# Hardware loops with lowered semaphores, and a first store in one piece, in a LayerNorm + GELU kernel

## The chip, the cores and the metric

The kernel runs on one core of a Trainium2 chip. The metric is the device time of one execution in microseconds (us), as a median over several executions. A profile of one execution shows each engine's instructions and each DMA packet; its span is 1.8 to 2.2 us shorter than the device time of that execution. The page is the profile's summary, and the chain is the work that ended last, followed back step by step to what released it. Engines: TensorE (PE, weight loads PEld), VectorE (DVE), ScalarE (ACT), GpSimd (POOL), SyncE (SP); a q behind a name is the engine's sequencer.

## The reference

The input `x` is 8 x 1024 rows of 2048 float32 values. Each row is normalised, scaled, shifted and put through the tanh form of GELU.

```python
mean = np.mean(x, axis=-1, keepdims=True)
var = np.var(x, axis=-1, keepdims=True)
normalized = (x - mean) / np.sqrt(var + eps)
out = gamma * normalized + beta
return (0.5 * out * (1 + np.tanh(np.sqrt(2 / np.pi) * (out + 0.044715 * out ** 3)))).astype(np.float32)
```

It reads 67.1 MB and writes 67.1 MB, and each value is used once.

## The kernel before

8192 rows make 64 tiles of 128 rows, in 16 batches of four tiles (4 MB). Five batch buffers go round. SyncE loads a batch as soon as the store from that buffer has landed. For each tile VectorE takes the statistics, GpSimd makes 1/sqrt(var + eps) and the shift from them, ScalarE normalises into bf16, VectorE multiplies by gamma, TensorE adds beta in PSUM (one matmul group puts beta there, the second adds the tile through an identity), and ScalarE applies GELU and writes over the batch buffer, which is then stored. All is unrolled in Python. The kernel's semaphores only rise, so each wait has its own number.

```python
def by_row(b):
    return b in (0, B - 1)            # first and last batch: stored as four 1 MB rows
# SyncE
for b in range(B):
    s = b % SLOTS
    if b >= SLOTS:
        prev = sum(16 * (R if by_row(c) else 1) for c in range(s, b, SLOTS))
        sy.wait_ge(s_store[s], prev)
    if b == 0:
        for q in range(R):
            sy.dma_start(out=xts[0][:, q:q + 1], in_=xg[0, :, q:q + 1]).then_inc(s_first[q], 16)
    else:
        sy.dma_start(out=xts[s], in_=xg[b]).then_inc(s_load[s], 16)
# ... GpSimd, unrolled over 64 tiles, three instructions each ...
# VectorE
for t in range(1, T):
    stats(t)          # four bn_stats, one bn_aggr
    scale(t - 1)      # times gamma; scale(0) first waits until gamma is spread: ve.wait_ge(s_c, 3)
scale(T - 1)
# ... ScalarE ...
# TensorE
for i in range(T):
    ps = pss[i % 2]
    for j in range(nsub):
        ins = pe.matmul(ps[:, cols(j)], lhsT=ones_b, rhs=b_hl[:, cols(j)], start=True, stop=False)
        if j == 0 and i >= 2:
            ins._wait_ge(s_g, i - 1)
    for j in range(nsub):
        ins = pe.matmul(ps[:, cols(j)], lhsT=ident, rhs=zgs[i % 2][:, cols(j)], start=False, stop=True)
        if j == 0:
            ins._wait_ge(s_v, v_scale(i))
    ins.then_inc(s_t, 1)
```

## Time and profile before

| | before |
|---|---|
| device time, median of 3 | 320.23 us (320.16 to 320.3) |
| span of the profile | 318.7 us |
| busiest engine | ScalarE, 79% |
| DMA, middle of the run | busy all the time, 425 to 432 GB/s |
| data moved | 134.36 MB in 6010 packets |
| pace of batches, loads at hand / in the long run | 16.4 / 19.4 us |

The prediction shows the lines behind this table and how they are read. In short: the DMA row has 9 (90% or more) in all slices but the ends, no engine has, and the waits are all of the kind "a buffer is not stored yet" or "a load is not here yet".

### The profile page before, as it was taken

The numbers are of one execution on the slowest core, as the hardware profiler recorded it, in microseconds if no ns is written. First come the engines' busy times: TensorE is split into PE (matmuls) and PEld (weight loads), VectorE is DVE, ScalarE is ACT, GpSimd is POOL, SyncE is SP. The second block draws the span as 40 slices with busy tenths as digits, with TensorE's granted clock in tenths as the row PEclk, the third lists the DMA queues.
The fourth block names the chain that finished last, engine by engine and source line by source line (L and its number), as shares of the span: only waits on it lengthen the run. The fifth ranks groups of instructions, "written<-read, shape, count | busy, mean of one in ns | idle before, by whom it ended". The sixth has DMA issues, their size and how long they took to land.

```text
span 318.7 us, 1855 instructions
## 1 busy us (share of the span) xinstructions
PE 241.2 (76%) x510; PEld 57.2 (18%) x520; DVE 249.1 (78%) x386; ACT 252.9 (79%) x132; POOL 115.1 (36%) x201
## 2 busy tenths in 40 slices
PE   2788889889989989785895868859687786768830
PEld 1211112222222222121121111112121121112100
DVE  3688999999999997996869868598786978968610
ACT  2779999999999999796896959949598696977850
POOL 1133444444444444333434424243232452433400
DMA  7999999999999999999999999999999999999995
GB/s 287 440 456 396 427 428 453 409 449 391 411 448 415 449 432 422 441 419 452 419 440 436 419 444 419 446 428 428 444 416 448 419 441 440 415 450 415 448 394 223
DMA packets 6010, 134.36 MB, mean 422 GB/s; under 512 B 704, under 2 KB 752, under 8 KB 752
## 3 DMA queue, kind: packets, MB, share of 16 engines
q1 hardware_dynamic: 2736, 67.11, 49.4%
q10 hardware_dynamic: 3264, 67.14, 49.1%
q8 instruction: 4, 0.07, 0.1%
q14 instruction: 6, 0.05, 0.0%
HBM read 67.13 MB, written 67.11 MB: 421 GB/s over the span
## 4 chain that ended last, share of the span: by engine, by line
DMA 63%; ACT 15%; DVE 9%; POOL 5%; PE 3%; issue 1%; ACTq 1%; SPq 0%
DMA out_dram<-xt 34%; DMA xt<-in_x_dram 27%; ACT yk L178 9%; DVE sts L143 6%; ACT xt L182 5%; POOL rss L131 3%; DVE zg L154 2%; PE ps L196 2%; DMA rows<-in_gamma_dram 2%; POOL ves L129 2%; POOL nms L133 1%; DVE mvs L149 1%; ACT g_t L175 1%; PE ps L210 1%; ACTq L187 0%
## 5 line engine op out<-in xcount | busy, mean ns | idle before, releaser
L143 DVE BATCH_NORM_STATS2 sts<-xt 128x6 f32<-128x512 f32 x256 | 157.7, 678 | 28.9 <-DMA xt<-in_x_dram 28.8
L178 ACT ACTIVATE yk<-xt,nms,rss 128x2048 bf16<-128x2048 f32 x64 | 133.9, 2092 | 44.9 <-POOL nms L133 39.9
L210 PE MATMUL ps<-zg,ident 128*128 128x512 bf16 x246 | 117.7, 627 | 57.2 <-DVE zg L154 55.6
L206 PE MATMUL ps<-b_hl,ones_b 33*128 33x512 bf16 x256 | 120.6, 624 | 2.0 <-ACT g_t L175 2.0
L182 ACT ACTIVATE xt<-ps 128x2048 f32<-128x2048 f32 x64 | 118.8, 1857 | 2.4 <-PE ps L210 2.4
L154 DVE TENSOR_TENSOR zg<-yk,g_t 128x2048 bf16<-128x2048 bf16 x64 | 77.3, 1208 | 20.8 <-ACT yk L178 20.8
L129 POOL TENSOR_SCALAR ves<-mvs 128x1 f32<-128x1 f32 x64 | 29.0, 454 | 172.9 <-DVE mvs L149 172.9
L131 POOL TENSOR_TENSOR rss<-ves,mhalf 128x1 f32<-128x1 f32 x64 | 55.5, 868 | 5.3
L210 PEld LDWEIGHTS ps<-zg,ident 128*128 128x128 bf16 x256 | 27.6, 130 | 147.3 <-DVE zg L154 112.0
L206 PEld LDWEIGHTS ps<-b_hl,ones_b 33*128 33x128 bf16 x256 | 27.1, 127 | 91.9 <-issue 88.4
L133 POOL TENSOR_SCALAR nms<-mvs,rss 128x1 f32<-128x1 f32 x64 | 29.6, 462 | 6.3
L149 DVE BATCH_NORM_AGGREGATE mvs<-sts 128x2 f32<-128x24 f32 x64 | 16.8, 263 | 2.2
L196 PE MATMUL ps<-rows,ones 1*128 1x512 f32 x8 | 7.2, 1072 | 6.1 <-DMA rows<-in_gamma_dram 6.1
L173 ACT ACTIVATE b_hl<-rows 1x2048 bf16<-1x2048 f32 x1 | 1.9, 1908 | 5.1 <-DMA rows<-in_beta_dram 5.1
L160 DVE TENSOR_TENSOR b_hl<-rows,b_hl 1x2048 bf16<-1x2048 f32 x1 | 2.3, 2280 | 2.5 <-ACT b_hl L174 2.5
L196 PEld LDWEIGHTS ps<-rows,ones 1*128 1x128 f32 x8 | 2.5, 322 | 9.3 <-DMA rows<-in_gamma_dram 6.1
L175 ACT ACTIVATE g_t<-ps 128x2048 bf16<-128x2048 f32 x1 | 1.9, 1877 | 2.2 <-PE ps L196 2.2
L169 ACT ACT_TABLE_LOAD x1 | 1.3, 1283 | 0.9 <-SPq L105 0.9
L174 ACT ACTIVATE b_hl<-rows 1x2048 bf16<-1x2048 f32 x1 | 1.9, 1908 | 0.0
L157 DVE MEMSET b_hl<- 33x1024 uint32 x1 | 0.9, 912 | 1.2 <-SPq L105 1.2
L121 POOL MEMSET ones<- 65x128 f32 x1 | 0.2, 201 | 0.5 <-SPq L105 0.5
L125 POOL TENSOR_SCALAR_AFFINE_SELECT ident<-ident 128x128 bf16<-128x128 bf16 x1 | 0.3, 292 | 0.1
(7 smaller groups left out, 0.9 us busy)
## 6 DMA issues: line engine op xcount, KB each, us to landing
xt<-in_x_dram SPq DMA_DIRECT2D x15, 4096.0 KB, 29.1
out_dram<-xt ACTq DMA_DIRECT2D x14, 4096.0 KB, 37.6
out_dram<-xt ACTq DMA_DIRECT2D x8, 1024.0 KB, 14.6
xt<-in_x_dram SPq DMA_DIRECT2D x4, 1024.0 KB, 8.4
rows<-in_beta_dram ACTq DMA_DIRECT2D x2, 8.0 KB, 5.8
rows<-in_gamma_dram ACTq DMA_DIRECT2D x1, 8.0 KB, 5.2
```

The source lines that it names most:

```text
L129: po.tensor_scalar(out=ves[:, c], in0=mvs[:, i, 1:2], scalar1=float(eps), scalar2=1.0, op0=ALU.add, op1=ALU.mult)._wait_ge(s_v, v_stats(i) ...
L131: po.tensor_tensor(out=rss[:, c], in0=ves[:, c], in1=mhalf, op=ALU.pow)._wait_ge(s_p, 3 * i + 1).then_inc(s_p, 1)
L133: po.tensor_scalar(out=nms[:, c], in0=mvs[:, i, 0:1], scalar1=rss[:, c], scalar2=-1.0, op0=ALU.mult, op1=ALU.mult)._wait_ge(s_p, 3 * i + 2 ...
L143: ins = ve.bn_stats(out=sts[:, i, j, :], in_=xr[:, j, :])
L149: ve.bn_aggr(out=mvs[:, i], in_=sts[:, i])._wait_ge(s_v, v_stats(i) - 1).then_inc(s_v, 1)
L154: ve.tensor_tensor(out=zgs[i % 2], in0=yks[i % 2], in1=g_t, op=ALU.mult)._wait_ge(s_n, i + 1).then_inc(s_v, 1)
L175: ac.activation(out=g_t, in_=pss[0], func=ACT.Identity)._wait_ge(s_tg, 1).then_inc(s_c, 1)
L178: ac.activation(out=yks[t % 2], in_=xrow(t), func=ACT.Identity, scale=rss[:, t:t + 1], bias=nms[:, t:t + 1])._wait_ge(s_p, 3 * t + 3).then ...
L182: ac.activation(out=xrow(i), in_=pss[i % 2], func=ACT.Gelu_apprx_tanh)._wait_ge(s_t, i + 1).then_inc(s_g, 1)
L196: ins = pe.matmul(pss[0][:, cols(j)], lhsT=ones[64:65], rhs=rows[64:65, j * K // nsub:(j + 1) * K // nsub, :d // K], start=True, stop=True)
L206: ins = pe.matmul(ps[:, cols(j)], lhsT=ones_b, rhs=b_hl[:, cols(j)], start=True, stop=False)
L210: ins = pe.matmul(ps[:, cols(j)], lhsT=ident, rhs=zgs[i % 2][:, cols(j)], start=False, stop=True)
```

## The change

Three engines no longer run straight-line code. VectorE loops 3 times over five batches, TensorE and GpSimd 16 times over one. A loop body has the same wait numbers in every turn, so a looped engine lowers the semaphores that it waits on by the count of the turn (VectorE a load's at once, the others at the end of the turn). The programme gets shorter; before fetches its instructions in ten packets (four on q8, six on q14), and the hope was for fewer. For five equal batches per turn the buffers are renumbered so that batch 0 stands alone. Two transfers change with it: the first batch is stored in one 4 MB piece, and batch 3 is loaded in four 1 MB pieces. From batch 1 on a load raises its semaphore by 64 in all. Cut to the core:

```diff
-        return b in (0, B - 1)
+        return b == B - 1                       # by_row
...
+                    elif b == SPLIT:            # SPLIT = 3
+                        sy.dma_start(out=xts[s][:, q:q + 1], in_=xg[b, :, q:q + 1]).then_inc(s_load[s], 16)
+                if b not in (0, SPLIT):
+                    sy.dma_start(out=xts[s], in_=xg[b]).then_inc(s_load[s], 16 * R)
...                                              # GpSimd
-        for i in range(T):
+            with po.Fori(0, B):
+                for k in range(R):
...
+                po.sem_inc(s_a, -R)
+                po.sem_inc(s_q, -2 * R)
...                                              # VectorE
+                if q == 0:
+                    ...
+                    ve.wait_ge(s_c, 3)
+                else:
+                    scale(q - 1, q)
...
+            with ve.Fori(0, (B - 1) // SLOTS):
+                for k in range(SLOTS * R):
+                    s, q = divmod(k, R)
+                    stats(s, q, (s_load[s], 16 * R) if q == 0 else None, k + 1)
+                    scale((q - 1) % R, k + 1)
+                ve.sem_inc(s_o, -SLOTS * R)
+                ve.sem_inc(s_n, -SLOTS * R)
...                                              # TensorE
+            pe.sem_inc(s_g, 2)
+            with pe.Fori(0, B):
+                for k in range(R):
...                                              # the eight matmuls as before
+                pe.sem_inc(s_g, -R)
+                pe.sem_inc(s_z, -R)
```

More of the change, by code (lines that the diff above doesn't have):

```diff
@@ L12 @@
 SLOTS = 5
+SPLIT = 3
+K = 16
 @with_exitstack
@@ L34 @@
     B = T // R
+    assert (B - 1) % SLOTS == 0
     xg = xf.rearrange("(b p r) d -> b p r d", p=P, r=R)
@@ L50 @@
     pss = [psum.tile([P, d], f32, name=f"ps{s}") for s in range(2)]
-    K = 16
     rows = sb("rows", [65, K, d // K + 4], f32)
@@ L58 @@
     g_t = sb("g_t", [P, d], bf16)
-    sts = sb("sts", [P, T, nsub, nc.vector.BN_STATS_DIM], f32)
-    mvs = sb("mvs", [P, T, 2], f32)
-    ves = sb("ves", [P, T], f32)
-    rss = sb("rss", [P, T], f32)
-    nms = sb("nms", [P, T], f32)
+    sts = sb("sts", [P, R, nsub, nc.vector.BN_STATS_DIM], f32)
+    mvs = sb("mvs", [P, R, 2], f32)
+    ves = sb("ves", [P, R], f32)
+    rss = sb("rss", [P, R], f32)
+    nms = sb("nms", [P, R], f32)
     def sem(name):
@@ L73 @@
     s_setp = sem("setp")
-    s_v = sem("v")
+    s_m = sem("m")
+    s_o = sem("o")
+    s_a = sem("a")
+    s_z = sem("z")
+    s_q = sem("q")
     s_p = sem("p")
@@ L77 @@
     s_g = sem("g")
+    s_r = sem("r")
     s_c = sem("c")
@@ L80, with slot @@
     s_tg = sem("tg")
-    def xrow(i):
-        return xts[i // R % SLOTS][:, i % R]
+    def slot(b):
+        return (b + SLOTS - 1) % SLOTS
     def row(p):
@@ L92, in cols @@
         return slice(j * FMAX, (j + 1) * FMAX)
-    def v_stats(t):
-        return 3 if t == 0 else 4 + 2 * t + (t - 1)
-    def v_scale(t):
-        return v_stats(t + 1) + 1 if t + 1 < T else v_stats(T - 1) + 2
     def by_row(b):
-        return b in (0, B - 1)
-    with tc.tile_critical():
-        sy = nc.sync
-        for b in range(B):
-            s = b % SLOTS
-            if b >= SLOTS:
-                prev = sum(16 * (R if by_row(c) else 1) for c in range(s, b, SLOTS))
-                sy.wait_ge(s_store[s], prev)
-            if b == 0:
-                for q in range(R):
-                    sy.dma_start(out=xts[0][:, q:q + 1], in_=xg[0, :, q:q + 1]).then_inc(s_first[q], 16)
-            else:
-                sy.dma_start(out=xts[s], in_=xg[b]).then_inc(s_load[s], 16)
-        po = nc.gpsimd
-        po.memset(ones, 1.0)
-        po.memset(ones_b, 1.0)
-        po.memset(mhalf, -0.5)
-        po.memset(ident, 0.0).then_inc(s_setp, 1)
-        po.affine_select(out=ident, in_=ident, compare_op=ALU.not_equal, fill=1.0, base=0,
-                         pattern=[[-1, P]], channel_multiplier=1)._wait_ge(s_setp, 1).then_inc(s_setp, 1)
-        for i in range(T):
-            c = slice(i, i + 1)
-            po.tensor_scalar(out=ves[:, c], in0=mvs[:, i, 1:2], scalar1=float(eps), scalar2=1.0,
-                             op0=ALU.add, op1=ALU.mult)._wait_ge(s_v, v_stats(i)).then_inc(s_p, 1)
-            po.tensor_tensor(out=rss[:, c], in0=ves[:, c], in1=mhalf,
-                             op=ALU.pow)._wait_ge(s_p, 3 * i + 1).then_inc(s_p, 1)
-            po.tensor_scalar(out=nms[:, c], in0=mvs[:, i, 0:1], scalar1=rss[:, c], scalar2=-1.0,
-                             op0=ALU.mult, op1=ALU.mult)._wait_ge(s_p, 3 * i + 2).then_inc(s_p, 1)
-        ve = nc.vector
-        def stats(i):
-            xr = xrow(i).rearrange("p (s f) -> p s f", f=FMAX)
-            b, q = divmod(i, R)
-            for j in range(nsub):
-                ins = ve.bn_stats(out=sts[:, i, j, :], in_=xr[:, j, :])
-                if j == 0 and b == 0:
-                    ins._wait_ge(s_first[q], 16)
-                elif j == 0 and q == 0:
-                    ins._wait_ge(s_load[b % SLOTS], 16 * (b // SLOTS + (b % SLOTS > 0)))
-            ins.then_inc(s_v, 1)
-            ve.bn_aggr(out=mvs[:, i], in_=sts[:, i])._wait_ge(s_v, v_stats(i) - 1).then_inc(s_v, 1)
-        def scale(i):
-            if i == 0:
-                ve.wait_ge(s_c, 3)
-            ve.tensor_tensor(out=zgs[i % 2], in0=yks[i % 2], in1=g_t,
-                             op=ALU.mult)._wait_ge(s_n, i + 1).then_inc(s_v, 1)
-        ve.memset(b_hl, 0.0).then_inc(s_v, 1)
-        stats(0)
-        ve.tensor_tensor(out=split(b_hl[32:33]), in0=row(32), in1=split(b_hl[32:33]),
-                         op=ALU.subtract)._wait_ge(s_c, 2).then_inc(s_v, 1)
-        for t in range(1, T):
-            stats(t)
-            scale(t - 1)
-        scale(T - 1)
-        ac = nc.scalar
-        ac.preload_act_table(ACT.Gelu_apprx_tanh)
-        for k, (p, src) in enumerate(((64, gamma), (0, beta), (32, beta))):
-            ac.dma_start(out=row(p), in_=src.rearrange("(o k f) -> o k f", o=1, k=K)).then_inc(s_par[k], 16)
-        ac.wait_ge(s_v, 1)
-        ac.activation(out=split(b_hl[0:1]), in_=row(0), func=ACT.Identity)._wait_ge(s_par[1], 16).then_inc(s_c, 1)
-        ac.activation(out=split(b_hl[32:33]), in_=row(32), func=ACT.Identity)._wait_ge(s_par[2], 16).then_inc(s_c, 1)
-        ac.activation(out=g_t, in_=pss[0], func=ACT.Identity)._wait_ge(s_tg, 1).then_inc(s_c, 1)
-        for t in range(T + 1):
-            if t < T:
-                ac.activation(out=yks[t % 2], in_=xrow(t), func=ACT.Identity, scale=rss[:, t:t + 1],
-                              bias=nms[:, t:t + 1])._wait_ge(s_p, 3 * t + 3).then_inc(s_n, 1)
-            i = t - 1
-            if i >= 0:
-                ac.activation(out=xrow(i), in_=pss[i % 2],
-                              func=ACT.Gelu_apprx_tanh)._wait_ge(s_t, i + 1).then_inc(s_g, 1)
-                b, q = divmod(i, R)
-                s = b % SLOTS
-                if by_row(b):
-                    ac.dma_start(out=og[b, :, q:q + 1],
-                                 in_=xts[s][:, q:q + 1])._wait_ge(s_g, i + 1).then_inc(s_store[s], 16)
-                elif q == R - 1:
-                    ac.dma_start(out=og[b], in_=xts[s])._wait_ge(s_g, i + 1).then_inc(s_store[s], 16)
-        pe = nc.tensor
-        pe.wait_ge(s_setp, 2)
-        for j in range(nsub):
-            ins = pe.matmul(pss[0][:, cols(j)], lhsT=ones[64:65],
-                            rhs=rows[64:65, j * K // nsub:(j + 1) * K // nsub, :d // K], start=True, stop=True)
-            if j == 0:
-                ins._wait_ge(s_par[0], 16)
-        ins.then_inc(s_tg, 1)
-        pe.wait_ge(s_c, 3)
-        pe.wait_ge(s_v, 4)
-        for i in range(T):
-            ps = pss[i % 2]
-            for j in range(nsub):
-                ins = pe.matmul(ps[:, cols(j)], lhsT=ones_b, rhs=b_hl[:, cols(j)], start=True, stop=False)
-                if j == 0 and i >= 2:
-                    ins._wait_ge(s_g, i - 1)
-            for j in range(nsub):
-                ins = pe.matmul(ps[:, cols(j)], lhsT=ident, rhs=zgs[i % 2][:, cols(j)], start=False, stop=True)
-                if j == 0:
-                    ins._wait_ge(s_v, v_scale(i))
-            ins.then_inc(s_t, 1)
-        for s in range(SLOTS):
-            sy.wait_ge(s_store[s], sum(16 * (R if by_row(c) else 1) for c in range(s, B, SLOTS)))
@@ new lines, in by_row, with stored, _, stats @@
+        return b == B - 1
+    def stored(b):
+        return sum(16 * (R if by_row(c) else 1) for c in range(b) if slot(c) == slot(b))
+    with tc.tile_critical(), nc.Block() as block:
+        @block.sync
+        def _(sy):
+            for b in range(B):
+                s = slot(b)
+                if stored(b):
+                    sy.wait_ge(s_store[s], stored(b))
+                for q in range(R):
+                    if b == 0:
+                        sy.dma_start(out=xts[s][:, q:q + 1], in_=xg[0, :, q:q + 1]).then_inc(s_first[q], 16)
+                    elif b == SPLIT:
+                        sy.dma_start(out=xts[s][:, q:q + 1], in_=xg[b, :, q:q + 1]).then_inc(s_load[s], 16)
+                if b not in (0, SPLIT):
+                    sy.dma_start(out=xts[s], in_=xg[b]).then_inc(s_load[s], 16 * R)
+            for b in range(B, B + SLOTS):
+                sy.wait_ge(s_store[slot(b)], stored(b))
+        @block.gpsimd
+        def _(po):
+            po.memset(ones, 1.0)
+            po.memset(ones_b, 1.0)
+            po.memset(mhalf, -0.5)
+            po.memset(ident, 0.0).then_inc(s_setp, 1)
+            po.affine_select(out=ident, in_=ident, compare_op=ALU.not_equal, fill=1.0, base=0,
+                             pattern=[[-1, P]], channel_multiplier=1)._wait_ge(s_setp, 1).then_inc(s_setp, 1)
+            with po.Fori(0, B):
+                for k in range(R):
+                    c = slice(k, k + 1)
+                    po.tensor_scalar(out=ves[:, c], in0=mvs[:, k, 1:2], scalar1=float(eps), scalar2=1.0,
+                                     op0=ALU.add, op1=ALU.mult)._wait_ge(s_a, k + 1).then_inc(s_q, 1)
+                    po.tensor_tensor(out=rss[:, c], in0=ves[:, c], in1=mhalf,
+                                     op=ALU.pow)._wait_ge(s_q, 2 * k + 1).then_inc(s_q, 1)
+                    po.tensor_scalar(out=nms[:, c], in0=mvs[:, k, 0:1], scalar1=rss[:, c], scalar2=-1.0,
+                                     op0=ALU.mult, op1=ALU.mult)._wait_ge(s_q, 2 * k + 2).then_inc(s_p, 1)
+                po.sem_inc(s_a, -R)
+                po.sem_inc(s_q, -2 * R)
+        @block.vector
+        def _(ve):
+            def stats(s, q, wait, count):
+                xr = xts[s][:, q].rearrange("p (s f) -> p s f", f=FMAX)
+                for j in range(nsub):
+                    ins = ve.bn_stats(out=sts[:, q, j, :], in_=xr[:, j, :])
+                    if j == 0 and wait:
+                        ins._wait_ge(*wait)
+                        if wait[0] is s_load[s]:
+                            ins.then_inc(s_load[s], -16 * R)
+                ins.then_inc(s_o, 1)
+                ve.bn_aggr(out=mvs[:, q], in_=sts[:, q])._wait_ge(s_o, count).then_inc(s_a, 1)
+            def scale(q, count):
+                ve.tensor_tensor(out=zgs[q % 2], in0=yks[q % 2], in1=g_t,
+                                 op=ALU.mult)._wait_ge(s_n, count).then_inc(s_z, 1)
+            ve.memset(b_hl, 0.0).then_inc(s_m, 1)
+            for q in range(R):
+                stats(slot(0), q, (s_first[q], 16), q + 1)
+                if q == 0:
+                    ve.tensor_tensor(out=split(b_hl[32:33]), in0=row(32), in1=split(b_hl[32:33]),
+                                     op=ALU.subtract)._wait_ge(s_c, 2).then_inc(s_m, 1)
+                    ve.wait_ge(s_c, 3)
+                else:
+                    scale(q - 1, q)
+            ve.sem_inc(s_o, -R)
+            ve.sem_inc(s_n, -(R - 1))
+            with ve.Fori(0, (B - 1) // SLOTS):
[5 more added lines that the diff above has]
+                ve.sem_inc(s_n, -SLOTS * R)
+            scale(R - 1, 1)
+        @block.scalar
+        def _(ac):
+            ac.preload_act_table(ACT.Gelu_apprx_tanh)
+            for k, (p, src) in enumerate(((64, gamma), (0, beta), (32, beta))):
+                ac.dma_start(out=row(p), in_=src.rearrange("(o k f) -> o k f", o=1, k=K)).then_inc(s_par[k], 16)
+            ac.wait_ge(s_m, 1)
+            ac.activation(out=split(b_hl[0:1]), in_=row(0), func=ACT.Identity)._wait_ge(s_par[1], 16).then_inc(s_c, 1)
+            ac.activation(out=split(b_hl[32:33]), in_=row(32),
+                          func=ACT.Identity)._wait_ge(s_par[2], 16).then_inc(s_c, 1)
+            ac.activation(out=g_t, in_=pss[0], func=ACT.Identity)._wait_ge(s_tg, 1).then_inc(s_c, 1)
+            for t in range(T + 1):
+                if t < T:
+                    b, q = divmod(t, R)
+                    ac.activation(out=yks[t % 2], in_=xts[slot(b)][:, q], func=ACT.Identity, scale=rss[:, q:q + 1],
+                                  bias=nms[:, q:q + 1])._wait_ge(s_p, t + 1).then_inc(s_n, 1)
+                i = t - 1
+                if i < 0:
+                    continue
+                b, q = divmod(i, R)
+                xt = xts[slot(b)]
+                ins = ac.activation(out=xt[:, q], in_=pss[i % 2], func=ACT.Gelu_apprx_tanh)._wait_ge(s_t, i + 1)
+                if by_row(b):
+                    ins.then_inc(s_r, 1)
+                    ac.dma_start(out=og[b, :, q:q + 1], in_=xt[:, q:q + 1])._wait_ge(
+                        s_r, b + q + 1).then_inc(s_store[slot(b)], 16)
+                    ac.sem_inc(s_g, 1)
+                elif q == R - 1:
+                    ins.then_inc(s_r, 1)
+                    ac.dma_start(out=og[b], in_=xt)._wait_ge(s_r, b + 1).then_inc(s_store[slot(b)], 16)
+                    ac.sem_inc(s_g, 1)
+                else:
+                    ins.then_inc(s_g, 1)
+        @block.tensor
+        def _(pe):
+            pe.wait_ge(s_setp, 2)
+            for j in range(nsub):
+                ins = pe.matmul(pss[0][:, cols(j)], lhsT=ones[64:65],
+                                rhs=rows[64:65, j * K // nsub:(j + 1) * K // nsub, :d // K], start=True, stop=True)
+                if j == 0:
+                    ins._wait_ge(s_par[0], 16)
+            ins.then_inc(s_tg, 1)
+            pe.wait_ge(s_c, 3)
+            pe.wait_ge(s_m, 2)
+            pe.sem_inc(s_g, 2)
+            with pe.Fori(0, B):
+                for k in range(R):
+                    ps = pss[k % 2]
+                    for j in range(nsub):
+                        ins = pe.matmul(ps[:, cols(j)], lhsT=ones_b, rhs=b_hl[:, cols(j)], start=True, stop=False)
+                        if j == 0:
+                            ins._wait_ge(s_g, k + 1)
+                    for j in range(nsub):
+                        ins = pe.matmul(ps[:, cols(j)], lhsT=ident, rhs=zgs[k % 2][:, cols(j)],
+                                        start=False, stop=True)
+                        if j == 0:
+                            ins._wait_ge(s_z, k + 1)
+                    ins.then_inc(s_t, 1)
+                pe.sem_inc(s_g, -R)
+                pe.sem_inc(s_z, -R)
```

## The prediction

> **What bounds the kernel now.** I read the page first: its engine shares, its 40 slices and its DMA queues.
>
> ```profile
> PE 241.2 (76%) x510; PEld 57.2 (18%) x520; DVE 249.1 (78%) x386; ACT 252.9 (79%) x132; POOL 115.1 (36%) x201
> ...
> DMA  7999999999999999999999999999999999999995
> ...
> DMA packets 6010, 134.36 MB, mean 422 GB/s; under 512 B 704, under 2 KB 752, under 8 KB 752
> ...
> q1 hardware_dynamic: 2736, 67.11, 49.4%
> q10 hardware_dynamic: 3264, 67.14, 49.1%
> q8 instruction: 4, 0.07, 0.1%
> q14 instruction: 6, 0.05, 0.0%
> ```
>
> No engine is over 79%, and the 16 DMA engines are at 9 in every slice but the first and the last. q1 is the loads, q10 the stores, q8 and q14 fetch instructions. The table by stage shows how hard the bound is: the DMA share is 1.00 in the middle, at 425 to 432 GB/s.
>
> ```profile
> 24.00:56.00 32.00, 27.65 (x60) 6.40 (x60) 29.02 (x46) 29.43 (x16) 14.25 (x23) 1.00 1.00 425
> 56.00:120.00 64.00, 56.88 (x122) 13.37 (x126) 59.73 (x95) 59.18 (x32) 27.57 (x47) 1.00 1.01 427
> 120.00:200.00 80.00, 61.72 (x134) 14.40 (x134) 64.65 (x102) 64.95 (x35) 30.83 (x51) 1.00 1.00 432
> 200.00:280.00 80.00, 60.05 (x130) 14.10 (x132) 62.95 (x100) 63.26 (x34) 29.15 (x50) 1.00 1.00 432
> ```
>
> In the packet records a 32 KB packet takes 1.213 us and an 8 KB packet 0.309 us on its engine. There are 1920 + 1792 of 32 KB and 512 + 1024 of 8 KB: (3712 x 1.213 + 1536 x 0.309) / 16 = 311.1 us. All packets together, with the slow ones, are 314.1 us on each engine; the first data packet starts at 1.9 us and the last ends at 317.0 us. So the span of 318.7 us is 1.9 of head, 314 of DMA work without a hole that I could find (no stretch of 4 us between 4 and 312 us lost more than 0.15 us), and some 2.5 us of uneven finish and completion.
>
> The waits say how much room the compute has.
>
> ```profile
> SPq L117 <- DMA out_dram<-xt: 245.6, 11, 58.1
> ...
> DVE sts L143 <- DMA xt<-in_x_dram: 28.8, 10, 3.8
> ```
>
> SyncE waits for stores to free buffers, and VectorE waits for loads. While loads lie ready, the batch stores are issued at 52.6, 69.3, 85.6, 101.9 and 118.3 us, 16.4 us apart. That is the pace of compute. From 136 us on they are 19.4 us apart, which is 8.39 MB at 432 GB/s, the pace of DMA. The slack is thus 3.0 us in each batch.
>
> The end of the chain, in order of time, gives the second number that matters.
>
> ```profile
> 254.36 29.12 DMA xt<-in_x_dram
> 283.48 0.02 issue
> 283.50 2.48 DVE sts L143 x4
> ...
> 306.57 1.88 ACT xt L182
> ```
>
> The last load lands at 283.5 us and the last GELU ends 25 us later, at 308.45. The last row's store needs 8 x 0.309 = 2.5 us of DMA[...]. It ends near 317 because it queues behind earlier stores. So the tail too is set by DMA[...].
>
> [...]from 24 to 56 us the loads (32 KB packets) move some 340 GB/s and the row stores (8 KB) some 80, about 4 to 1; later, with equal packets, both get about 215. [...] The trace shows the blocks as q8 packets of 16 KB, four, 65 to 77 us apart (16 tiles of 16 TensorE instructions), and 8 KB ones on q14[...]. [...]
>
> **The change, part by part.**
>
> *Transfers.* The first store becomes one piece (four 8 KB-packet stores become one of 32 KB packets), and the load of batch 3 is cut into four (the reverse). 8 KB packets: loads 1024, stores 512, again 1536 in all; 32 KB again 3712. The sum stays 311.1 us: **0 us**.
>
> *Order of transfers.* The first store is issued at about 36 us, where its fourth row was, not 22.5. Until then loads run alone, 9.8 us a batch (measured 13.1 to 22.9 us for the second): three batches by 32.7 us, half of batch 3 by 37.5. Then a 32 KB store runs against 8 KB loads, 4 to 1, and needs 9.7 x 5/4 = 12.1 us: done by about 50 us, where the row stores ended at 62.5. Load 5 is issued near 51 instead of 63.4. Batch 3 is loaded by 52 us; store 1 begins at 54 and shares evenly with load 4, done by about 70; load 5, 19.4 us later, by about 89 (before: 87.3 by bytes). DMA has work throughout. All later loads move by some +2 us, the last one to land near 285.5. [...]**0 us**.
>
> *Loops.* VectorE turns back twice, TensorE and GpSimd 15 times. A turn is two semaphore instructions and a branch[...]. TensorE idles 57.2 us before its second matmul group, 0.9 us a tile, and GpSimd 172.9 us in 64 waits, 2.7 us; most of that covers a turn, and the 3.0 us slack per batch covers the rest: **0 us**. VectorE's body is 20 tiles x 6 = 120 instructions[...], with about 28 before it. Its 8 KB fetches before were at 42.9, 132.4 and 232.4 us (by their spacing of some 21 tiles); at 42.9 it was about 50 instructions in. [...]
>
> *Fewer fetches.* A fetch takes 0.31 us (8 KB) or 0.88 to 0.97 us (16 KB) on one DMA engine, and the next packet there took 0.4 to 0.55 us too long: 0.85 to 1.4 us each. [...] Four TensorE and about two GpSimd fetches go; one or two VectorE ones may come. I judge **-0.7 us** from the difference between engines that fetched 16 KB (ending 315.4 to 315.9) and most others (314.3 to 314.8); matching packets to engines was not certain.
>
> *Entry and exit.* [...] The extra issues on SyncE fall after enough is queued.
>
> Sum: 320.23 - 0.7 + 0.2, rounded to **319.7 us**.
>
> **Rivals.** [...] (2) The shifted order makes the last load later than I worked out[...] and compute ends the kernel: +1 to +3 us, 322 us. For it: the tail is short of spare time. Against it: +2 us is what the order gives. (3) All fetch delay falls away and the engines end level near 314.5: -2 us, 318 us. Against it: ScalarE remains unrolled and still fetches.
>
> **Range and chances.** Rivals 2 and 3 make the ends: **318.2 to 321.8 us**. Faster by 2% is under 313.8, below head plus DMA work, which the change leaves alone: 0.01. Slower by 2% is over 326.6, rival 1: 0.04. Same: 0.95.
>
> **What would show it.** Right: DMA at 9 in all slices but the ends; 6010 packets again; q8 with no or one fetch; the first store issued near 36 us, load 5 near 51; the last load landing at 285 to 286; the last GELU ending near 310 with stores still queued. Wrong: a gap in DMA or under 425 GB/s in the middle; TensorE idle for 3 us and more at the start of each batch; store issues more than 19.4 us apart; or a last store that starts as soon as it is issued.

The sum: 320.23 - 0.7 + 0.2 = 319.73, rounded to 319.7 us; the +0.2 us was for entry and exit, a guess that no trace gave. Rival 1, by which TensorE waits for instructions at every turn, is cut too; the 0.04 for "slower" rested on it. The blocks on q8 and q14 are the packets that the page calls instruction.

## The result and the profile after

The changed kernel took 320.65 us (median of 4 runs, 320.52 to 320.87), against 320.26 us for before beside it. The ratio is 1.0011 with a 95% interval of 0.9994 to 1.0028: the same. In two later comparisons the changed kernel was 0.06 us above and 0.09 us below before. The 0.5 us of gain that I had forecast did not come in any of the three.

The page of the changed kernel's profile, in the parts that answer to those shown of before:

```profile
PE 244.4 (77%) x520; PEld 57.2 (18%) x520; DVE 247.5 (78%) x386; ACT 251.7 (79%) x132; POOL 110.5 (35%) x201
...
DMA  7999999999999999999999999999999999999994
...
DMA packets 6002, 134.26 MB, mean 421 GB/s; under 512 B 704, under 2 KB 752, under 8 KB 752
...
q1 hardware_dynamic: 3168, 67.11, 49.4%
q10 hardware_dynamic: 2832, 67.13, 48.9%
q14 instruction: 2, 0.02, 0.0%
```

The busy times of the engines and the DMA row are nearly those of before. The packets only changed sides: 432 fewer on the stores' queue, 432 more on the loads', where the split first store and the now split load hand over 4 x 128 - 128 data packets and 3 x 16 small ones. The ten instruction fetches (q8 and q14) became two; the 6010 packets that I had named as a sign had not taken off these eight.

The stages of 24 to 56 and 56 to 120 us, in the columns of the prediction's table (the last two are the DMA share and GB/s):

```profile
24.00:56.00 32.00, 29.07 (x64) 6.55 (x61) 29.62 (x47) 29.67 (x16) 13.60 (x24) 1.00 1.00 414
56.00:120.00 64.00, 57.94 (x126) 13.53 (x127) 59.60 (x96) 59.11 (x32) 26.80 (x46) 1.00 1.00 433
```

Before had 425 and 427 GB/s there: the changed kernel moves less in the first stage, with DMA just as busy, and more in the second.

The waits of SyncE and VectorE of the changed kernel (total us, times, longest):

```profile
SPq L121 <- DMA out_dram<-xt: 241.4, 11, 46.6
...
DVE sts L151 <- DMA xt<-in_x_dram: 30.7, 11, 3.5
```

These are the waits of before with nearly the same totals (245.6 and 28.8 us). And the chain at its end, in order of time (start, duration, what):

```profile
251.85 31.78 DMA xt<-in_x_dram
283.64 0.03 issue
...
283.73 2.48 DVE sts L151 x4
...
307.04 1.88 ACT xt L204
```

The last load landed at 283.6 us (283.5 before) and the last GELU ended at 308.9 us (308.45 before). The load of batch 5 was issued at 53.3 us, where I had worked out 51 and before had 63.4.

Such a "same" can be nothing plus nothing, or a gain and a loss that meet. The experiments had to tell which.

### The profile page after: what moved, and what is told of

Read it like the earlier page. It is cut to its first block, busy times and chain, and to the rows that moved or that the text cites. A ratio compares the mean times of both kernels' runs of the same rounds, so it can differ in the third digit from the quotient of the medians.

```text
span 318.6 us, 2087 instructions
## 1 busy us (share of the span) xinstructions
PE 244.4 (77%) x520; PEld 57.2 (18%) x520; DVE 247.5 (78%) x386; ACT 251.7 (79%) x132; POOL 110.5 (35%) x201
## 4 chain that ended last, share of the span: by engine, by line
DMA 63%; ACT 14%; DVE 10%; POOL 5%; PE 3%; issue 1%; ACTq 0%; DVEq 0%; POOLq 0%; SPq 0%
DMA out_dram<-xt 31%; DMA xt<-in_x_dram 30%; ACT yk L197 9%; DVE sts L151 7%; ACT xt L204 4%; POOL ves L137 3%; DVE zg L160 2%; PE ps L222 2%; POOL rss L139 2%; DMA rows<-in_gamma_dram 2%; DVE mvs L157 1%; POOL nms L141 1%; PE ps L239 1%; ACT g_t L193 1%; ACTq L207 0%
## 5 line engine op out<-in xcount | busy, mean ns | idle before, releaser
L151 DVE BATCH_NORM_STATS2 sts<-xt 128x6 f32<-128x512 f32 x256 | 157.7, 679 | 32.1 <-DMA xt<-in_x_dram 30.7
L239 PE MATMUL ps<-zg,ident 128*128 128x512 bf16 x256 | 120.8, 627 | 54.6 <-DVE zg L160 53.5
L137 POOL TENSOR_SCALAR ves<-mvs 128x1 f32<-128x1 f32 x64 | 37.4, 585 | 177.9 <-DVE mvs L157 177.9
L160 DVE TENSOR_TENSOR zg<-yk,g_t 128x2048 bf16<-128x2048 bf16 x64 | 76.5, 1195 | 19.0 <-ACT yk L197 19.0
L139 POOL TENSOR_TENSOR rss<-ves,mhalf 128x1 f32<-128x1 f32 x64 | 37.1, 580 | 5.3
L141 POOL TENSOR_SCALAR nms<-mvs,rss 128x1 f32<-128x1 f32 x64 | 34.9, 546 | 6.3
```

The lines of the kernel that those rows point to most:

```text
L137: po.tensor_scalar(out=ves[:, c], in0=mvs[:, k, 1:2], scalar1=float(eps), scalar2=1.0, op0=ALU.add, op1=ALU.mult)._wait_ge(s_a, k + 1).the ...
L139: po.tensor_tensor(out=rss[:, c], in0=ves[:, c], in1=mhalf, op=ALU.pow)._wait_ge(s_q, 2 * k + 1).then_inc(s_q, 1)
L141: po.tensor_scalar(out=nms[:, c], in0=mvs[:, k, 0:1], scalar1=rss[:, c], scalar2=-1.0, op0=ALU.mult, op1=ALU.mult)._wait_ge(s_q, 2 * k + 2 ...
L151: ins = ve.bn_stats(out=sts[:, q, j, :], in_=xr[:, j, :])
L160: ve.tensor_tensor(out=zgs[q % 2], in0=yks[q % 2], in1=g_t, op=ALU.mult)._wait_ge(s_n, count).then_inc(s_z, 1)
L239: ins = pe.matmul(ps[:, cols(j)], lhsT=ident, rhs=zgs[k % 2][:, cols(j)], start=False, stop=True)
```

## The experiments

The theory was that DMA packets set the time, that their number and sizes have not changed, and that turns of the loops are hidden. Rivals: the new transfers cost something and the loops win it back; or the turns cost something. A third question was whether a turn of a loop can wait for its own instructions.

### One part of the change at a time

The new transfers on the unrolled kernel:

```diff
-        return b in (0, B - 1)
+        return b == B - 1
...
+            elif b == SPLIT:
+                for q in range(R):
+                    sy.dma_start(out=xts[s][:, q:q + 1], in_=xg[b, :, q:q + 1]).then_inc(s_load[s], 16)
```

> The unrolled kernel of before with the new transfers alone: first store in one piece, load of batch 3 in four. Theory (DMA packets set the time, their number and sizes are the same): 320.3 us, within 0.3 us of before; load 5 issued near 53 us, last load landing near 283.6 us, instruction packets on q8 four as before. Rival (the new order costs the 0.4 us that the changed kernel seems slower by, and the loops cost nothing): 320.6 to 320.7 us.

Measured: 320.76 us against 320.45 us for before on the same chip. Four of the six runs lie from 320.62 to 320.8; two took 322.98 and 324.77 us, for which no profile shows a reason, and they pull the ratio of the means to 1.0048 (1.0009 to 1.0086). So 0.3 us by the medians: the rival's side, not mine, though barely.

The loops with the transfers of before:

```diff
-SPLIT = 3
+SPLIT = 0                                  # batch 3 in one piece
...
-        return b == B - 1
+        return b in (0, B - 1)             # first batch in four rows
```

> The changed kernel with the transfers of before: first batch stored in four rows, batch 3 loaded in one piece. Theory: 320.3 us, within 0.3 us of before; load 5 issued near 63 us again; two or three instruction packets. Rival (the loops cost the 0.4 us): 320.6 to 320.7 us. A third (the missing instruction fetches are worth what I predicted, and the new order gives it back): 319.6 us.

Measured: 319.77 us, ratio 0.9981 (0.9968 to 0.9994). The third possibility came true: the loops are worth 0.7 us, and the new transfers give it back. The page of this kernel:

```profile
DMA packets 6002, 134.26 MB, mean 422 GB/s; under 512 B 704, under 2 KB 752, under 8 KB 752
...
q1 hardware_dynamic: 2736, 67.11, 49.3%
q10 hardware_dynamic: 3264, 67.14, 49.1%
q14 instruction: 2, 0.02, 0.0%
```

The data queues have exactly the packets of before; only the instruction queues differ, two fetches in place of ten.

> The changed kernel itself once more, as control on this chip beside the others. Theory: no difference to before that clears the noise, 320.3 to 320.7 us. Rival: a steady 0.4 us over before, with an interval that leaves out 1.

Measured: 320.51 us, ratio 1.0003 (0.999 to 1.0015). The 0.4 us of the first comparison was not steady. On this chip the changed kernel is 0.74 us slower than the loops alone. It is also only 0.25 us faster than the unrolled kernel with the same new transfers (320.76 us), which is within the spread of the runs: beside the new transfers the loops win less.

### How much room compute has

Three more statistics instructions in one tile of each looped batch (results unused):

```diff
+                if q == 1 and wait is None:
+                    for m in range(3):
+                        ve.bn_stats(out=more[:, m, :], in_=xr[:, m % nsub, :])
```

> The changed kernel with three more statistics instructions on VectorE in one tile of each looped batch, some 1.9 us a batch. Theory (3.0 us of slack in each batch, DMA is the bound): the time stays within 0.7 us of the changed kernel, 320.6 to 321.3 us, and the time VectorE waits for loads falls from 30.7 us to under 10 us. Rival (a stall of compute shows in the time one for one): 15 batches x 1.9 = 28 us more, 349 us.

Measured: 320.93 us, 0.42 us above the changed kernel beside it. The first line is the page's engine shares, the next two are VectorE's waits.

```profile
PE 244.3 (77%) x520; PEld 57.2 (18%) x520; DVE 273.0 (86%) x431; ACT 250.7 (79%) x132; POOL 111.1 (35%) x201
...
DVE zg L164 <- ACT yk L201: 19.4, 32, 3.1
DVE sts L155 <- DMA xt<-in_x_dram: 5.0, 2, 3.8
```

VectorE works 25.5 us longer, and its wait for loads falls from 30.7 to 5.0 us: almost one for one. In the trace batches follow each other at 18.15 us from the second to the last but one, and the last one is scaled at 290.9 us, where the changed kernel of the first profile had 290.8. The slack is real: 1.8 of its 3.0 us a batch were spent, some 25 us in all, and the time rose by no more than the runs of either kernel spread (320.41 to 321.31 and 320.31 to 321.03 us).

### The cost of a turn by itself

The full kernel can hide what loops cost, for its VectorE waits 30.7 us for loads. So I cut the stores: of every batch but the last only the fourth row is stored. The result is wrong. DMA work falls to some 220 us (77% of 286.2 us by the unrolled kernel's page) and compute sets the time: VectorE waits for a load only once, at the start (3.8 us unrolled, 3.7 with loops).

```diff
-                    ac.dma_start(out=og[b], in_=xt)
+                    ac.dma_start(out=og[b, :, q:q + 1], in_=xt[:, q:q + 1])
```

> A wrong result on purpose: of each batch but the last only the fourth row is stored, a quarter of the bytes, so that DMA work falls to some 200 us and compute is the bound. Unrolled, with the new transfers. Theory: batches 16.4 us apart from first to last, the whole near 27 + 14 x 16.4 + 25 + 6 + 1.6 = 289 us, DMA share well under 0.9. It is the base for the next three; no rival.

> The same cut in stores on the changed kernel, with its loops and lowered semaphores. Theory ([...]most of it under waits that the engine has anyway): within 3 us of the unrolled one. Rival (turns stand on the chain of compute in full): [...]. Second rival (a turn waits for an instruction block): [...]15 or more instruction packets.

Measured: 287.77 us unrolled, 289.18 us with loops, 1.4 us more (1.25 in the two profiled runs). The DMA share was not "well under 0.9", as I had expected, but 0.92 and 0.86 in the unrolled kernel (56 to 120 and 120 to 200 us) and 0.88 and 0.89 in the other. Still, in neither do the times of batches grow apart: the step from batch to batch is 16.36 to 16.39 us in both, but for the first of the 15 in the unrolled kernel (16.84). The 16 turns together cost nothing that can be seen. What differs stands at the ends. With loops the first scaling starts at 18.0 us, unrolled at 17.3: the change has moved VectorE's wait for gamma ahead of the second tile's statistics, and in the full kernel too its waits show

```profile
DVE sts L151 <- ACT g_t L193: 1.4, 1, 1.4
```

which before does not have. The last GELU ends 0.73 us later. From the last data packet to the end of the device time the profiled runs take 4.08 us with loops and 3.55 us unrolled, so another 0.5 us belongs to the way out.

A turn is not free on its engine. TensorE's last four instructions of a turn in the looped kernel with cut stores (count, duration in ns as least, median and greatest, times of the first and the last):

```profile
L244 PEldq EVENT_SEMAPHORE  x16: 51/51/51, 31.8 to 277.8; - x16
...
L231 PEldq ALU_OP  x16: 36/36/42, 32.1 to 278.1; - x16
L231 PEldq COMPARE_BRANCH  x16: 76/208/232, 32.2 to 278.2; - x16
```

From the first of the two semaphore instructions to the end of the branch one turn takes 0.61 us on TensorE (113.62 to 114.23), 0.35 us on VectorE and 0.27 us on GpSimd. In the trace of the changed kernel the branch alone takes 208 ns on TensorE, 67 ns on VectorE and 45 ns on GpSimd (medians). TensorE waits in any case for VectorE in nearly every tile (85.0 us in all for its weight loads), and the next run shows whether the turn disappears there.

> As the last, but TensorE's loop has 4 turns of 16 tiles (256 TensorE instructions in the body) instead of 16 turns of 4. Theory (TensorE's turns are hidden under its wait for VectorE): within 1 us of the kernel with 16 turns, no more instruction packets. Rival (TensorE's turns cost on the path): faster[...]. [...]

Measured: 289.25 us, against 289.18 with 16 turns. TensorE's turns cost nothing that can be seen; the theory holds.

For the last of the four, two batches stand ahead of TensorE's loop:

```diff
+            for k in range(2 * R):
+                ...                            # the eight matmuls, waits on k + 1
+            pe.sem_inc(s_g, -2 * R)
+            pe.sem_inc(s_z, -2 * R)
-            with pe.Fori(0, B):
+            with pe.Fori(0, B - 2):
```

> As the second, but TensorE's first two batches stand ahead of its loop[...]. Theory[...]: an instruction packet of 16 KB on q8 or more in each of 13 turns[...]. Rival[...]: no more than one or two q8 packets and the same time within 1 us.

The question: a fetch at each turn or none.

Measured: 289.16 us. The instruction queues of the page:

```profile
q8 instruction: 1, 0.02, 0.0%
q14 instruction: 2, 0.02, 0.0%
```

One 16 KB fetch, at 59.8 us, in the first pass, and none in 13 turns. The same holds for the kernel with 4 turns, whose body has 256 TensorE instructions: one fetch at 61.4 us. So no turn of any size tried here waited for instructions. Which instructions a packet holds is not settled: it shows when they were fetched, no more.

### Which transfer it is

The last four runs stood beside each other, all with loops. Two corners of the square each undo one of the two transfers (`by_row` alone, or `SPLIT` alone, as in the diff above).

> The changed kernel, with batch 3 loaded in one piece again; the first store stays in one piece. Theory (the 8 KB load packets that run against the first 32 KB store take up to twice as long, near 0.8 us on each DMA engine between 36 and 45 us, and that is the cost of the new transfers): the excess there falls under 0.2 us and the time to 319.8 us, 0.6 us below the changed kernel beside it. Rival (the first store's later start, and with it the later last load, costs): 320.4 us, no change.

> The changed kernel, with the first batch stored row by row again; batch 3 stays loaded in four pieces. Theory: 8 KB loads and 8 KB stores meet evenly; if it is the meeting with a 32 KB store that slows the 8 KB loads, no excess and 319.8 us; if 8 KB loads are slow beside any store, an excess of 0.5 us and more between 24 and 60 us and 320.3 us. Rival (the first store's later start costs): 319.8 us in either case.

> The loops with both transfers of before once more, as the base of this comparison. Theory: 319.8 us again, 0.5 to 0.7 us below the changed kernel and 0.6 us below before, with an interval that leaves out 1. Rival (the first result was chance): 320.3 us.

> The changed kernel as the fourth corner. Theory: 320.5 us, within 0.3 us of before, 0.6 us above the loops with the old transfers. Rival: under 320.1 us, so that the new transfers cost nothing.

Measured, with the packet records beside it. "Excess" is the sum of what packets took over 1.213 us (32 KB) or 0.309 us (8 KB), divided by 16 engines, for packets that start between 24 and 45 us, which is when the first store begins.

| kernel | first store | load of batch 3 | time, us | excess 24 to 45 us | last load lands | last GELU ends |
|---|---|---|---|---|---|---|
| loops, old transfers, again | four rows | one piece | 319.94 (319.76 to 320.2) | 0.45 | 281.6 | 307.4 |
| loops, one-piece store only | one piece | one piece | 320.3 (320.15 to 320.51) | 0.77 | 279.3 | 305.1 |
| loops, split load only | four rows | four pieces | 320.35 (320.26 to 320.52) | 0.79 | 283.2 | 308.9 |
| changed kernel, third | one piece | four pieces | 320.38 (320.28 to 320.45) | 0.72 | 286.0 | 311.6 |

Before beside them took 320.47 us. The loops with the old transfers are again ahead of it, by a ratio of 0.9977 (0.9957 to 0.9998); two of the eleven runs of before were slow (321.27 and 322.23 us, unexplained), and by the medians the gain is 0.53 us. My theory falls in its form. Without any 8 KB load of batch 3 the excess stays at 0.77 us, and undoing the split alone wins 0.1 us. The rival falls as well: with the one-piece store alone the last load lands earliest of all, and the time is still 320.3. Either of the two transfers alone costs some 0.4 us, and both together no more than that. What goes with the time, in this window, is the excess at the onset of the stores, nearly all of it on packets of the loads: 0.28 and 0.45 us in the two profiles of the loops with old transfers and 0.33 in before, 0.72 to 0.96 in the three profiles of the changed kernel and 0.81 in the unrolled one with new transfers. That is a coincidence of sizes over nine profiles, and no run here took the excess away by itself. A longer window undoes it: with both old transfers the packets lose more after 56 us. From 24 to 120 us the same sum is 0.76 and 1.13 us for the loops with old transfers, 1.36 for before, 0.86 and 0.89 with one transfer undone, 0.94 to 1.11 for the changed kernel and 0.97 for the unrolled one with new transfers. That is no order of the times any more. So neither what makes the new transfers cost 0.4 us nor why packets slow down is shown.

## Why the prediction was right or wrong

**The bound and the result: right.** I put 319.7 us with 318.2 to 321.8 and a chance of 0.95 for "same"; it was 320.65 us. The result lay 0.95 us above my middle. "Same" was safe, since the change leaves the 314 us of DMA work alone; the forecast inside it, 0.5 us faster, did not come (0.39 us slower, then 0.06 slower and 0.09 faster), because terms of both signs below were mis-sized.

**"Transfers: 0 us": wrong in size.** The step counted packets, and the count was right (3712 of 32 KB and 1536 of 8 KB in both profiles). It took each packet to last the same in any order. The new transfers cost 0.74 us with loops on one chip, 0.44 us on another and 0.3 us unrolled. This is the term that moved the result above my middle most. What in the transfers costs it stays open: the slower onset of the stores has the size, but is made up for by 120 us.

**"Order of transfers": right in the middle, past its limit at the end in two of three profiles.** Load 5 went out at 53.3 us (worked out: 51) and its bytes were there at 88.0 us (89). For the last load I had 285.5 us: the three profiles of the changed kernel have 283.6, 286.8 and 286.3 us. I had counted on spare time in the tail, by an estimate: no trace showed all its parts. In two of the three profiles nothing was left. The chain of the second one:

```profile
250.88 35.95 DMA xt<-in_x_dram
...
286.92 2.48 DVE sts L151 x4
...
310.23 1.88 ACT xt L204
```

The chain's last load lands 3.2 us later than in the first profile, and the last GELU ends at 312.1 us. (The table above gives the last small packet of the load, 286.0 us in the third profile, and the chain the wait's end, 286.3.) Each transfer has 16 small packets (704 in 44 transfers), and those of that load show why: the median one was done at 282.2 us and the last one only at 286.5. The last store then ends at 316.9 us with all 16 engines within 0.6 us of each other, so here compute ends the kernel, as in rival 2, and the sign of being wrong that I had named, a last store that starts as soon as it is issued, came true. The spare time was also less than I had counted: from the last GELU's end to the landing of a store that does not queue took 5.1 us (312.1 to 317.2), about twice the 2.5 us that its packets need. In the first profile one engine ended 2 us after the rest. Both ends come to within half a microsecond, which is why the time hardly tells them apart. Another sign also came true, under 425 GB/s in the middle: 414, 418 and 421 in the three profiles from 24 to 56 us. It tells little, for the loops with old transfers have 421 and 420 there.

**"Loops: 0 us": right, and for a stronger reason.** I had set turns against idle time and slack. The kernel with cut stores has little of that slack and still keeps 16.37 us a batch. A turn takes 0.61 us on TensorE and 0.35 us on VectorE. No fetch came at a turn of VectorE: the changed kernel fetched at 46.9 and 105.3 us and turned at 108.0 and 202.1. The second fetch is probably ScalarE's: with the old transfers, where only ScalarE and SyncE have other instructions, it comes at 91.7 us.

**"Fewer fetches, -0.7 us": of the right size, cause not isolated.** The loops with old transfers took 0.68 us and 0.53 us less than before beside them; with the new transfers, which is the case that I had predicted, they took 0.25 us less. At the last data packet, before the exit, the loops are 0.9 to 1.1 us ahead with the old transfers (315.8 and 316.1 against 316.95 us) and 0.2 to 0.7 with the new (316.4 to 316.9 against 317.07). Fetches fell from ten to two with data packets unchanged. In before the ten took 5.5 us of DMA time and I find six packets behind them that took 2.8 us too long, together 0.5 us on each of 16 engines (an estimate from these packets). The fetches are the likeliest cause but not the only difference: the loops also brought lowered semaphores, loads that count 64 and the moved wait. So this is left open.

**Entry and exit, the +0.2 us of the sum: too small, at the exit.** The term was a guess. The first data packet starts at 1.9 us in all kernels. From the last data packet to the end of the device time the two unrolled kernels with whole stores took 3.55 us each, and the eight with loops 4.0 to 4.4, in the median 4.0: some +0.45 us, as with cut stores (3.55 and 4.08). The moved wait came to 0.65 us with cut stores; what it costs in the full kernel no run shows.

The sum in hindsight: about -0.6 for the loops, their exit included, and +0.4 to +0.7 for the transfers. The version to keep is the loops with the old transfers, 319.77 and 319.94 us, faster than both kernels by 0.1 to 0.2%.

## What to carry to other kernels

When DMA is busy from end to end, count the packets first: here a change that left their number and sizes alone moved the time by less than 1 us either way. To see what a loop's turn costs, shrink the transfers until compute is the bound; here TensorE's turns vanished (289.25 us with 4, 289.18 with 16) under waits that the engine had anyway (85.0 us). A result of "same" from a change with several parts is worth taking apart, for here a part that wins 0.2% was hidden by one that loses it. And test a suspected cause over the whole run: a loss that fits the time in one window can be made up in the next.
